# Prompt attention of a two-layer decoder step: transposes by half rows, the mask in the evictions, fixed engine orders

## The chip, the cores and the metric

The kernel runs on one core of a Trainium2 chip. The metric is the time of one execution on the device in microseconds (us); smaller is better. The kernel before the change took 3136.19 us (median of three runs, 3132.84 to 3143.44).

## The reference

One inference step of a small decoder for two groups of requests: one prompt of 1024 tokens behind 16 meta tokens, and eight samples of eight tokens each. Layer one is an mLSTM mixer, layer two a "forgetting attention" that reads one shared K and V; each is followed by a SwiGLU feed-forward part. The change touches the attention of the prompt alone:

```
# q, k, v: (1, 1040, 16 heads, 64); c = cumsum(log forget gate) over the positions
def one_block(qi, ci, pi):              # a block of 128 queries
    s = einsum('bqhd,bkhd->bhqk', qi, k)
    s = s + ci[..., None] - c[:, :, None, :]
    s = where(pos_k <= pi[:, None], s, -inf)
    return einsum('bhqk,bkhd->bqhd', softmax(s), v)
out = (o * sigmoid(og)) @ w_out
```

All data are float32. Only the 1024 prompt queries are computed in this stage; the queries of the 16 meta tokens come from the stage before.

## The kernel before

The program goes through the stages of both layers one after another; `attend_prompt` is the stage between the sample attention (`attend_sample`, with the sigmoid gates of the output as filler on TensorE) and the last output projection with its feed-forward part (`mlp`). q, k, the values, the negated decay sums `cD` and the gates `og2D` lie in DRAM scratch when it starts.

The 16 heads go in eight pairs `hp`: partitions 0 to 63 hold one head's 64 features, 64 to 127 the other's (`z` = 0, 1). The 1024 queries go in four groups `g` of two blocks `u` of 128, in the order `QG = (0, 3, 1, 2)`. Block `qb = 2g + u + 1` sees its first 16 + 128 qb keys; their last 128 are the diagonal.

Scores (`scores`, L1731 on). A block's keys are cut in pieces by `KSPLIT`, for example (400, 384) for `qb` 6. A piece is three matmuls per head (high times high, high times low, low times high part of q and k, L1751) into one PSUM bank per head, `sp0` and `sp1`, one place each. The piece with the diagonal gets two more matmuls per head (L1757), which add a mask of minus 1e30 through an identity. VectorE then evicts each head's piece with one instruction (L1759): it adds the decay row `ncb`, writes the score row `s` and carries the running maximum in `mx`. GpSimd makes the bias `nb` (L1768, L1769), ScalarE takes the exponential in place with the row sum in `sm` (L1771).

Products (`units`, L1775 on). A unit takes two columns of 128 keys (the last unit of a group: one, and the rest). Its first half, `turn`, transposes the 128x128 tiles of `s` on TensorE into PSUM (L1793, L1799), two units deep, and ScalarE copies them to `th` (L1796, L1807). In the last unit of a group the last 16 keys of each row are transposed from 32 partitions (L1803) and copied by VectorE (L1808). Its second half, `prod`, multiplies with the values into the bank `po` (L1816, L1820, and over 16 partitions L1824); at the end of a group VectorE makes the reciprocal `r` of the row sums (L1828), TensorE spreads it (L1831), VectorE multiplies by gate and `r` (`y`, L1834, L1835), and GpSimd splits the result in two parts for the next projection (L1843, L1844).

Order. TensorE's order is written out by hand (`manual_schedule` for TensorE): `ahead` keeps the score pieces nine pieces and more ahead of the products that use them, and per unit come score pieces, `turn`, score pieces, and the `prod` of the unit before. Below, S is a score piece, T a `turn`, P a `prod`. The order on VectorE, ScalarE and GpSimd is left to the framework's scheduler. `load` (L1709 on) brings a head pair's nine operands by SyncE's queue, into tiles that alternate between two places. At the start the last gate (`last_gate`, L1687 on) fills TensorE between the first nine score pieces.

Of the kernel before, what the change touches and what calls it, by code (L numbers as in the profile page):

```python
# [1667 lines left out]
def attend_prompt(self, ys):  # L1668
# [3 lines left out]
    with self.pool("ap", bufs=1) as sp, self.pool("ap2", bufs=2) as s2, self.pool("app", bufs=2, space=PSUM) as pp:  # L1672


        mask = sp.tile([P, 2, P], F32R, name="mneg")
        idr = sp.tile([P, 2, P], F32R, name="idr")
        tmp = sp.tile([P, 2, P], F32, name="mtmp")
        for dst, fill, op, sign in ((mask, NEG, ALU.is_ge, -1), (idr, 1.0, ALU.not_equal, -1)):
            nc.gpsimd.memset(tmp, 0.0)
            for a in range(2):  # L1680
                for h in range(2):
                    x = tmp[a * 64 : a * 64 + 64, h, :]
                    nc.gpsimd.affine_select(out=x, in_=x, compare_op=op, fill=fill, base=h * 64, pattern=[[sign, P]],
                                            channel_multiplier=1)
            nc.vector.tensor_copy(dst, tmp)

        def last_gate():  # L1687

            for t, (t0, t1) in enumerate(TS):
                n = t1 - t0  # L1690
                ps = pp.tile([P, 512], F32, name=f"og7{t}", tag="op")
# [4 lines left out]
                s = s2.tile([P, SL], F32, name=f"og7s{t}", tag="og7", bufs=1)  # L1696
                nc.scalar.activation(s[:, :n], ps[:, :n], AF.Sigmoid)
                nc.gpsimd.dma_start(self.og2D[7, :, t0:t1], s[:, :n])

        def first_tile():  # L1700

            og0 = sp.tile([P, KT, T0], F32, name="og0")
            nc.sync.dma_start(og0, self.og2D[:, :, :T0].rearrange("m p t -> p m t"))
            nc.vector.tensor_tensor(out=ys, in0=ys, in1=og0, op=ALU.mult)
            self.split(ys, self.X[0][0][:, :, :T0], self.X[0][1][:, :, :T0])

        heads = {}

        def load(hp):  # L1709
            cs = slice(hp * P, hp * P + P)  # L1710
            vr = s2.tile([P, 9, P], F32, name=f"vr{hp}", tag="vr")
            og = s2.tile([P, SEQ], F32, name=f"og{hp}", tag="ogP")
            kq = []
            for nm, d in (("q", self.qD), ("k", self.kD)):
                for z in range(2):
                    t = s2.tile([P, NP], F32R, name=f"{nm}{z}_{hp}", tag=f"{nm}{z}")
                    nc.sync.dma_start(t.bitcast(F32), d[z][hp])
                    kq.append(t)
            ncb = []
            for z in range(2):  # L1720
                t = s2.tile([P, NP], F32, name=f"ncb{z}_{hp}", tag=f"ncb{z}")
                nc.sync.dma_start(t, self.cD[2 * hp + z].partition_broadcast(P))
                ncb.append(t)
            nc.sync.dma_start(vr[:, :8, :], self.vD[: 8 * P, cs].rearrange("(j p) d -> p j d", p=P))
            nc.sync.dma_start(vr[:NM, 8, :], self.vD[8 * P :, cs])
            nc.sync.dma_start(og, self.og2D[hp, :, T0:])
            heads[hp] = (kq, ncb, vr, og)
# [3 lines left out]
        def scores(hp, g):  # L1731

            (qh, ql, kh, kl), ncb, _, _ = heads[hp]
            sm = s2.tile([P, 2, 2], F32, name=f"sm{hp}_{g}", tag="sm", bufs=4)
            ss = {}
            rows[hp, g] = (ss, sm)
            for u in range(2):
                qb = 2 * g + u + 1
                nk = NM + P * qb
                qs = slice(NM + P * (qb - 1), NM + P * qb)  # L1740
                for z in range(2):
                    ss[z, u] = s2.tile([P, nk], F32, name=f"s{hp}_{qb}_{z}", tag=f"s{qb}")
                mx = s2.tile([P, 2, 4], F32, name=f"mx{hp}_{qb}", tag="mx", bufs=4)
                at = 0
                for c, n in enumerate(KSPLIT[qb]):
                    ps = [pp.tile([P, 512], F32, name=f"sp{hp}_{qb}_{c}_{z}", tag=f"sp{z}", bufs=1) for z in range(2)]
                    diag = at + n == nk
                    for x, (a, b) in enumerate(((qh, kh), (qh, kl), (ql, kh))):
                        for z in range(2):
                            r = slice(z * 64, z * 64 + 64)  # L1750
                            nc.tensor.matmul(ps[z][:, :n], a[r, qs], b[r, at : at + n], start=(x == 0),  # L1751
                                             stop=(x == 2 and not diag))
                    if diag:
                        for x in range(2):
                            for z in range(2):
                                r = slice(z * 64, z * 64 + 64)
                                nc.tensor.matmul(ps[z][:, n - P : n], idr[r, x], mask[r, x], start=False, stop=(x == 1))  # L1757
                    for z in range(2):
                        nc.vector.tensor_tensor_reduce(  # L1759
                            out=ss[z, u][:, at : at + n], in0=ps[z][:, :n], in1=ncb[z][:, at : at + n], scale=1.0,  # L1760
                            scalar=NEG if c == 0 else mx[:, z, c - 1 : c], op0=ALU.add, op1=ALU.max,
                            accum_out=mx[:, z, c : c + 1])
                    at += n
                    if diag:

                        nb = s2.tile([P, 2], F32, name=f"nb{hp}_{qb}", tag="nb", bufs=4)
                        cq = self.cqP[:, qb - 1, 2 * hp : 2 * hp + 2]
                        nc.gpsimd.tensor_tensor(out=nb, in0=cq, in1=mx[:, :, c], op=ALU.subtract)  # L1768
# [6 lines left out]
        def units(hp, g):  # L1775

            _, _, vr, og = heads[hp]
            ss, sm = rows[hp, g]
            po = pp.tile([P, 512], F32, name=f"op{hp}_{g}", tag="op")
            nf = 2 * g + 1  # L1780
            out = []
            for j0 in range(0, nf, 2):
# [3 lines left out]
                def turn(j0=j0, tail=tail, hold=hold):  # L1786
                    pt = pp.tile([P, 2, 2, 256], F32, name=f"tp{hp}_{g}_{j0}", tag="tp")
                    th = s2.tile([P, 2, 2, 256], F32, name=f"th{hp}_{g}_{j0}", tag="th", bufs=3)
                    hold["th"] = th
                    for x in range(1 if tail else 2):  # L1790
                        for z in range(2):
                            for u in range(2):
                                nc.tensor.transpose(pt[:, x, z, u * P : u * P + P],  # L1793
                                                    ss[z, u][:, (j0 + x) * P : (j0 + x + 1) * P], self.ident)
                    if not tail:
                        nc.scalar.copy(th, pt)  # L1796
                        return
                    for z in range(2):
                        nc.tensor.transpose(pt[:, 1, 0, z * P : z * P + P], ss[z, 1][:, nf * P : (nf + 1) * P],  # L1799
                                            self.ident)  # L1800
                    for z in range(2):
                        for u in range(2):
                            nc.tensor.transpose(pt[:NM, 1, 1, (2 * z + u) * 32 : (2 * z + u) * 32 + 32],  # L1803
                                                ss[z, u][96:, (nf + u) * P : (nf + u) * P + NM],
                                                self.ident[96:, 96:])
# [125 lines left out]
```

## Time and profile before

| what | us |
| --- | --- |
| median of three runs | 3136.19 |
| the profiled execution, device time | 3134.74 |
| its span, first to last instruction | 3133.0 |
| prompt attention, first score matmul to last y product | 1892.8 to 2205.7 |

The profile shows one execution. A row of a timeline has the start in us from the span's start, the time covered, engine, line, instruction, tiles, shapes and count, and in brackets the idle time before it with what ended it. Neighbouring instructions of one kind are merged into one row, so the time covered reaches from the first one's start to the last one's end, and matmuls overlap in it. PE is TensorE, PEld its weight loads, DVE VectorE, ACT ScalarE, POOL GpSimd, SPq SyncE's DMA issues. A row of groups has busy time and mean duration in ns, then the idle time before. A row of waits has the total, the number and the longest.

In the stage TensorE's row is full: of the 40 us from 1972 to 2012 it is busy for 40.00, VectorE for 19.78, ScalarE for 23.87, GpSimd for 8.26, and the granted clock is 1.00.

### The profile page before, as it was taken

The numbers are of one execution on the slowest core, as the hardware profiler recorded it, in microseconds if no ns is written. First come the engines' busy times: TensorE is split into PE (matmuls) and PEld (weight loads), VectorE is DVE, ScalarE is ACT, GpSimd is POOL, SyncE is SP. The second block draws the span as 40 slices with busy tenths as digits, with TensorE's granted clock in tenths as the row PEclk, the third lists the DMA queues.
The fourth block names the chain that finished last, engine by engine and source line by source line (L and its number), as shares of the span: only waits on it lengthen the run. The fifth ranks groups of instructions, "written<-read, shape, count | busy, mean of one in ns | idle before, by whom it ended". The sixth has DMA issues, their size and how long they took to land.

```text
span 3133.0 us, 50924 instructions
## 1 busy us (share of the span) xinstructions
PE 3034.0 (97%) x21182; PEld 2883.1 (92%) x21182; DVE 1265.6 (40%) x2678; ACT 950.2 (30%) x1873; POOL 412.2 (13%) x806
## 2 busy tenths in 40 slices
PE   7999989999999999999999998999999999999998
PEld 7998879999999999999999886777999999999998
DVE  5132545633333333272455433554453333333323
ACT  5122453311111111142445445666331111111112
POOL 2011322100000000044453011222210000000002
PEclk9999999999999999999999998999999999999999
DMA  6142544111111111134444854332311111111111
GB/s 212 33 117 82 140 120 123 47 48 41 45 43 41 48 41 48 41 112 141 152 156 126 297 207 167 110 124 75 113 48 41 47 41 43 45 41 48 41 41 58
DMA packets 243314, 277.85 MB, mean 89 GB/s; under 512 B 26510, under 2 KB 193866, under 8 KB 243082
## 3 DMA queue, kind: packets, MB, share of 16 engines
q1 hardware_dynamic: 215426, 195.88, 19.9%
q0 software_dynamic: 23984, 76.40, 7.5%
q8 instruction: 166, 2.72, 0.4%
q10 hardware_dynamic: 3672, 2.31, 0.3%
q14 instruction: 66, 0.54, 0.1%
HBM read 211.35 MB, written 63.18 MB: 88 GB/s over the span
## 4 chain that ended last, share of the span: by engine, by line
PE 79%; DVE 4%; ACT 2%; DMA 2%; issue 1%; POOL 0%; SPq 0%; ACTq 0%; DVEq 0%; POOLq 0%
PE fps L63 11%; PE fps L62 11%; PE fps L64 11%; PE dps L62 5%; PE dps L63 5%; PE dps L64 5%; PE tmps L62 3%; PE tmps L63 3%; PE tmps L64 3%; PE sp L1751 3%; PE tp L1793 2%; PE op L1816 2%; PE pops L64 2%; PE pops L63 2%; PE pops L62 2%
## 5 line engine op out<-in xcount | busy, mean ns | idle before, releaser
L133 DVE TENSOR_TENSOR slot<-slot,slot 128x1024 fp32r<-128x1024 f32 x140 | 171.9, 1229 | 483.7 <-ACT slot L132 483.6
L132 ACT CAST slot<-slot 128x1024 fp32r<-128x1024 f32 x140 | 147.1, 1051 | 707.9 <-PE dps L63 393.7
L62 PE MATMUL dps<-ah,slot 128*128 128x384 f32 (+1 forms) x1056 | 353.1, 334 | 6.1 <-DVE vA L1075 3.1
L63 PE MATMUL dps<-al,slot 128*128 128x384 f32 (+1 forms) x1056 | 349.1, 331 | 0.0
L64 PE MATMUL dps<-ah,slot 128*128 128x384 f32 (+1 forms) x1056 | 348.7, 330 | 0.0
L205 POOL TENSOR_TENSOR ns<-ns,nq 128x384 f32<-128x384 f32 (+1 forms) x72 | 80.9, 1123 | 1717.6 <-ACT nq L203 1717.5
L62 PE MATMUL fps<-x1h,slot 128*128 128x384 f32 x704 | 236.9, 337 | 0.0
L62 PE MATMUL fps<-x2h,slot 128*128 128x384 f32 x704 | 236.5, 336 | 0.0
L63 PE MATMUL fps<-x2l,slot 128*128 128x384 f32 x704 | 236.5, 336 | 0.0
L64 PE MATMUL fps<-x2h,slot 128*128 128x384 f32 x704 | 236.5, 336 | 0.0
L64 PE MATMUL fps<-x1h,slot 128*128 128x384 f32 x704 | 236.5, 336 | 0.0
L63 PE MATMUL fps<-x1l,slot 128*128 128x384 f32 x704 | 236.4, 336 | 0.0
L64 PE MATMUL fps<-x0h,slot 128*128 128x336 f32 x704 | 223.0, 317 | 0.0
L62 PE MATMUL fps<-x0h,slot 128*128 128x336 f32 x704 | 222.5, 316 | 0.0
L63 PE MATMUL fps<-x0l,slot 128*128 128x336 f32 x704 | 222.4, 316 | 0.0
L62 PEld LDWEIGHTS dps<-ah,slot 128*128 128x128 f32 x1056 | 198.3, 188 | 13.9 <-DVE vA L1075 6.6
L63 PEld LDWEIGHTS dps<-al,slot 128*128 128x128 f32 x1056 | 198.5, 188 | 0.2
L64 PEld LDWEIGHTS dps<-ah,slot 128*128 128x128 f32 x1056 | 198.3, 188 | 0.0
L1053 DVE TENSOR_TENSOR fs<-fps,fs 128x336 f32<-128x336 f32 x132 | 71.4, 541 | 282.7 <-PE fps L64 282.7
L1075 DVE TENSOR_TENSOR Ht<-Ht,dps 128x384 f32<-128x384 f32 (+1 forms) x240 | 125.7, 536 | 106.0 <-PE dps L64 106.0
L1075 DVE TENSOR_TENSOR vA<-vA,dps 128x384 f32<-128x384 f32 (+1 forms) x240 | 125.4, 535 | 91.2 <-PE dps L64 91.2
L132 ACT CAST ah<-fs 128x336 fp32r<-128x336 f32 x132 | 65.7, 498 | 282.0 <-DVE fs L1053 282.0
(560 smaller groups left out, 7335.2 us busy)
## 6 DMA issues: line engine op xcount, KB each, us to landing
slot<-in_w_gate_up SPq DMA_DIRECT2D x88, 512.0 KB
slot<-in_w_down SPq DMA_DIRECT2D x44, 512.0 KB
kp<-in_cache_k SPq DMA_DIRECT2D x32, 512.0 KB
vp<-in_cache_v SPq DMA_DIRECT2D x32, 512.0 KB
wraw<-in_w_in_a SPq DMA_DIRECT2D x24, 512.0 KB
ncb<-cD SPq DMA_DIRECT2D x16, 520.0 KB
slot<-in_w_qo_b SPq DMA_DIRECT2D x16, 512.0 KB
slot<-in_w_kvf SPq DMA_DIRECT2D x14, 512.0 KB
```

Of the source, the lines that this page charges most:

```text
L62: mm(ps, sh, mh, start=first, stop=False)
L63: mm(ps, sh, ml, start=False, stop=False)
L64: mm(ps, sl, mh, start=False, stop=last)
L132: self.nc.scalar.copy(hi, src)
L133: self.nc.vector.tensor_tensor(out=lo, in0=src, in1=hi.bitcast(F32), op=ALU.subtract)
L205: (nc.vector if x == KT - 1 else nc.gpsimd).tensor_tensor(out=s, in0=s, in1=sq, op=ALU.add)
L1053: nc.vector.tensor_tensor(out=s[:, :n], in0=ps[:, :n], in1=s[:, :n], op=ALU.mult)
L1075: nc.vector.tensor_tensor(out=H[t][:, m], in0=H[t][:, m], in1=o, op=ALU.add)
L1751: nc.tensor.matmul(ps[z][:, :n], a[r, qs], b[r, at : at + n], start=(x == 0), stop=(x == 2 and not diag))
L1793: nc.tensor.transpose(pt[:, x, z, u * P : u * P + P], ss[z, u][:, (j0 + x) * P : (j0 + x + 1) * P], self.ident)
L1816: mm(po[ds[z], :256], vr[:, j0 + x, ds[z]], th[:, x, z], start=(j0 + x == 0), stop=False)
```

## The change

- Every 128x128 transpose becomes two of 64 rows by 128 columns, the upper and the lower half of the queries, which write to two PSUM banks. One ScalarE copy takes both banks to `th`.
- The four matmuls of the mask go. A tile `nd` holds the last 128 decay values of a block plus the mask; GpSimd makes it three blocks ahead (`masked`). The piece with the diagonal is evicted in two instructions per head, the part before the diagonal and the diagonal.
- The last 16 keys: the small transposes become ordinary matmuls over 64 partitions with a part of the identity; ScalarE copies them into `tails`, zero below row 16; values and weights are then multiplied over all 128 partitions.
- Three score places shared by both heads instead of one each; one product bank instead of two.
- VectorE, ScalarE and GpSimd are ordered by hand as well: they take their instructions in the order of the text.
- `load` is split into `load_k` (q, k, decay) and `load_v` (values, gates in quarters), issued at other points; the first tiles are allocated ahead in a set order; the last gate uses the places of `tp` and `th`; the gating of the sample rows (`first_tile`) is split in two calls; `y` is written over the gate.

```diff
+        tails = [sp.tile([P, P], F32, name=f"tail{x}") for x in range(2)]
...
+        def load_k(hp, e):
+            kq = first.pop(0) if first else place_k(hp)
+            ncb = firstc.pop(0) if firstc else place_c(hp)
+            for t, d in zip(kq, (self.qD[0], self.kD[0], self.kD[1], self.qD[1])):
+                e.dma_start(t.bitcast(F32), d[hp])
+            e.dma_start(ncb, self.cD[2 * hp : 2 * hp + 2].partition_broadcast(P))
+            heads[hp] = (kq, ncb)
...
+        def load_v(hp, e):
             cs = slice(hp * P, hp * P + P)
...
+            e.dma_start(vr[:, :8, :], self.vD[: 8 * P, cs].rearrange("(j p) d -> p j d", p=P))
+            nc.gpsimd.memset(vr[:, 8, :], 0.0)
+            e.dma_start(vr[:NM, 8, :], self.vD[8 * P :, cs])
...
+        def masked(x):
+            if x < len(blocks):
+                hp, qb = blocks[x]
+                d = diag[x] = s2.tile([P, 2, P], F32, name=f"nd{hp}_{qb}", tag="nd", bufs=4) if x else nd
+                nk = NM + P * qb
+                nc.gpsimd.tensor_tensor(out=d, in0=heads[hp][1][:, :, nk - P : nk],
+                                        in1=mask.unsqueeze(1).broadcast_to([P, 2, P]), op=ALU.add)
...
+                x = blocks.index((hp, qb))
+                masked(x + 3)
...
+                    ps = [pp.tile([P, 512], F32, name=f"sp{hp}_{qb}_{c}_{z}", tag="sp", bufs=3) for z in range(2)]
...
-                    if diag:
-                        for x in range(2):
-                            for z in range(2):
-                                r = slice(z * 64, z * 64 + 64)
-                                nc.tensor.matmul(ps[z][:, n - P : n], idr[r, x], mask[r, x], start=False, stop=(x == 1))
+                    parts = [(0, n)] if at + n < nk else [(0, n - P), (n - P, n)]
                     for z in range(2):
...
+                        for y, (o, e) in enumerate(parts):
+                            nc.vector.tensor_tensor_reduce(
+                                out=ss[z, u][:, at + o : at + e], in0=ps[z][:, o:e],
+                                in1=diag[x][:, z] if y else ncb[:, z, at + o : at + e], scale=1.0,
+                                scalar=mx[:, z, c + y - 1 : c + y] if c + y else NEG, op0=ALU.add, op1=ALU.max,
+                                accum_out=mx[:, z, c + y : c + y + 1])
...
+            po = pp.tile([P, 512], F32, name=f"op{hp}_{g}", tag="op", bufs=1)
...
+                    for y, (z, u, j) in enumerate(ts):
+                        for h in range(2):
+                            r = slice(h * 64, h * 64 + 64)
+                            nc.tensor.transpose(pt[:, h, y], ss[z, u][r, j * P : j * P + P], self.ident[r, r])
+                    if tail:
                         for z in range(2):
                             for u in range(2):
+                                nc.tensor.matmul(pt[:NM, 1, 6 + z, u * 32 : u * 32 + 32],
+                                                 ss[z, u][64:, (nf + u) * P : (nf + u) * P + NM],
+                                                 self.ident[64:, 96:], start=True, stop=True)
+                    n = len(ts)
+                    nc.scalar.copy(th.rearrange("p x z (u h q) -> p h (x z u) q", h=2, q=64)[:, :, :n], pt[:, :, :n])
+                    if tail:
+                        nc.scalar.copy(tw[:NM], pt[:NM, 1, 6:].rearrange("p a q -> p (a q)"))
...
+                            mm(po[ds[z], u * P + 96 : u * P + P], vr[:, nf + u, ds[z]], tw[:, c : c + 32],
                                start=False, stop=(u == 1))
...
-        with tc.manual_schedule(engines={mybir.EngineType.PE}):
-            load(0)
+        with tc.manual_schedule(engines={E.PE, E.DVE, E.Activation, E.Pool}):
```

More of the change, by code (lines that the diff above doesn't have):

```diff
@@ L1672, in attend_prompt @@
     with self.pool("ap", bufs=1) as sp, self.pool("ap2", bufs=2) as s2, self.pool("app", bufs=2, space=PSUM) as pp:
[L1675 to L1685, printed above, removed]
+        mask = sp.tile([P, P], F32, name="mneg")
+        nc.gpsimd.memset(mask, 0.0)
+        nc.gpsimd.affine_select(out=mask, in_=mask, compare_op=ALU.is_ge, fill=NEG, base=0, pattern=[[-1, P]],
+                                channel_multiplier=1)
+        tails = [sp.tile([P, P], F32, name=f"tail{x}") for x in range(2)]
+        for x in tails:
+            nc.gpsimd.memset(x, 0.0)
+        nd = s2.tile([P, 2, P], F32, name="nd0", tag="nd", bufs=4)
+        w7f = [w.bitcast(F32).rearrange("p k n -> p (k n)") for w in self.w7]
         def last_gate():
@@ L1739, in scores @@
                 nk = NM + P * qb
+                x = blocks.index((hp, qb))
+                masked(x + 3)
                 qs = slice(NM + P * (qb - 1), NM + P * qb)
                 for z in range(2):
[L1742 to L1748, printed above, removed]
+                    ss[z, u] = firsts.pop((qb, z)) if (qb, z) in firsts else row(hp, qb, z)
@@ L1795, in turn @@
[L1795 to L1805, printed above, removed]
@@ L1875, in attend_prompt @@
             for hp, g in groups:
-                if g == QG[0] and hp < 7:
-                    load(hp + 1)
                 us = None
```

111 lines of the change are left out of this document (65 added, 46 removed).

## The prediction

> **What bounds the kernel now.** I read the page first.
>
> ```profile
> PE 3034.0 (97%) x21182; PEld 2883.1 (92%) x21182; DVE 1265.6 (40%) x2678; ACT 950.2 (30%) x1873; POOL 412.2 (13%) x806
> ```
>
> TensorE is busy nearly throughout, but this is an average over stages. The prompt attention is the stretch in which the lines of the change run. Its length per pair of heads ("a head pair", eight of them) comes from the timeline of SyncE: the same load is issued once per head pair.
>
> ```profile
> 1972.81 0.32 SPq L1717 DMA_DIRECT2D q<-qDh  x1
> 2008.40 0.32 SPq L1717 DMA_DIRECT2D q<-qDh  x1
> ```
>
> That is 35.6 us per head pair, 285 us for eight. Inside one, the timeline of 2000 to 2012 us shows the blocks S (a score piece), T (the transposes of one unit) and P (the products of one unit):
>
> ```profile
> 2000.08 0.81 PE L1751 MATMUL sp<-k,q 64*128 64x400 f32 x6
> ...
> 2000.82 1.09 PE L1793 MATMUL tp<-ident,s 128*128 128x128 f32 x8
> ...
> 2001.84 0.85 PE L1751 MATMUL sp<-k,q 64*128 64x256 f32 x5
> ...
> 2002.91 0.65 PE L1816 MATMUL op<-th,vr 128*64 128x256 f32 x4
> ...
> 2003.39 0.39 PE L1820 MATMUL op<-th,vr 128*64 128x128 f32 x4
> ...
> 2003.71 0.42 PE L1824 MATMUL op<-th,vr 16*64 16x32 f32 x8
> ...
> 2004.06 0.66 PE L1831 MATMUL op<-ident,r 128*64 128x128 f32 x8
> ...
> 2004.65 1.09 PE L1793 MATMUL tp<-ident,s 128*128 128x128 f32 x8
> ...
> 2007.43 1.12 PE L1751 MATMUL sp<-k,q 64*128 64x384 f32 x6
> ...
> 2008.22 0.50 PE L1757 MATMUL sp<-mneg,idr 64*128 64x128 f32 x4
> ...
> 2008.65 1.09 PE L1793 MATMUL tp<-ident,s 128*128 128x128 f32 x8
> ...
> 2009.67 1.08 PE L1816 MATMUL op<-th,vr 128*64 128x256 f32 x8
> ...
> 2010.69 0.56 PE L1751 MATMUL sp<-k,q 64*128 64x144 f32 x6
> ...
> 2011.08 0.38 PE L1757 MATMUL sp<-mneg,idr 64*128 64x128 f32 x4
> ...
> 2011.39 0.66 PE L1793 MATMUL tp<-ident,s 128*128 128x128 f32 x4
> ```
>
> A block's price is the distance from its start to the next block's. No block waits long for another engine: TensorE's own sequence sets the pace. Eight transposes take 1.02 us from start to next block; their own row, less the last one's tail of 0.27 us, gives some 0.11 us between starts, 0.87 for eight. The other 0.15 us is the entry into a block of another array shape (128*128 after 64*128). Whether the 64-row matmuls of S run two abreast, a full-array stream of about the same width shows:
>
> ```profile
> 1909.06 0.33 PE L64 MATMUL og<-x1h,wlo 128*128 128x384 f32 x1
> 1909.23 0.33 PE L62 MATMUL og<-x1h,whi 128*128 128x384 f32 x1
> ```
>
> One costs 0.17 us, so six in a row 1.0 us; the six of 400 columns at 2000.08 took 0.74. They do run in pairs, three times 0.175, and 0.21 us is the entry into S.
>
> **The change on TensorE, per head pair.** Counting the emission order of the loops (unchanged): 72 tiles of 128x128 are transposed, 8 blocks of scores end in a mask, 4 groups have a last unit, and on average T follows S 5.6 times and S follows T 7.4 times.
>
> - Half rows: 72 tiles at 0.11 become 72 pairs of 64 columns, 0.055 if the halves run abreast as S's do. Saved 3.9; bounds 0 (no overlap) and 3.9.
> - T takes S's array shape, so entries between them go: 5.6 x 0.15 + 7.4 x 0.21 = 2.4. From S or T into P and out they stay.
> - Masks off TensorE: four matmuls took 0.31 us at 2011.08 with T's entry, about 0.2 without; eight blocks, 1.6.
> - Last keys in full rows: L1820 and L1824 take 0.32 and 0.35 us, each with a shape change behind it; in one shape 0.21 and 0.22. That and the shape change inside T save 1.4 for four groups; the small transposes as full fp32 products (two passes) give 0.5 back. Net 0.9.
>
> Together 8.8 us. Three score places can also take the present waits for a free place:
>
> ```profile
> PEld sp L1751 <- DVE mx L1759: 8.5, 38, 0.6
> ```
>
> This is the view of waits of 1932 to 2200 us, total, times and longest: 1.1 us per head pair. With everything else hidden, a head pair would take 35.6 - 8.8 - 1.1 = 25.7 us.
>
> **What is late next.** VectorE, ScalarE and GpSimd now take their work in the order of the text. These rows show what that moves:
>
> ```profile
> 2008.66 0.62 DVE L1759 CUSTOM_DVE_ANT_0 s<-sp,ncb,mx 128x384 f32<-128x384 f32 x1 [0.95 <-PE sp L1751]
> ...
> 2009.20 0.61 DVE L1759 CUSTOM_DVE_ANT_0 s<-sp,ncb,mx 128x384 f32<-128x384 f32 x1
> ...
> 2009.74 0.09 DVE L1759 DVE_READ_ACCUMULATOR2_ANT mx<- 128x1 f32 x1
> 2009.84 1.01 ACT L1796 COPY th<-tp 128x1024 f32<-128x1024 f32 x1 [2.72 <-PE tp L1793]
> ...
> 2010.24 0.20 POOL L1769 TENSOR_TENSOR nb<-nb,cqP 128x2 f32<-128x2 f32 x1
> ...
> 2010.74 0.95 ACT L1771 ACTIVATE s<-s,nb 128x784 f32<-128x784 f32 x1
> ```
>
> The T block of 2008.65 is copied out at 2009.84, ahead of the two exponentials of the S block that TensorE did before it. In the text those exponentials stand first. In fixed order the copy starts when they end: S ends at 2008.66; evictions, maximum and bias take until 2010.44, 1.8 us; two exponentials 1.9; the copy 1.0; 4.7 in all. The diagonal now has an eviction of its own for each head. What that costs comes from
>
> ```profile
> 2011.59 0.31 DVE L1759 CUSTOM_DVE_ANT_0 s<-sp,ncb 128x144 f32<-128x144 f32 x1 [1.77 <-issue]
> ...
> 2011.82 0.30 DVE L1759 CUSTOM_DVE_ANT_0 s<-sp,ncb 128x144 f32<-128x144 f32 x1
> ```
>
> 0.23 us apart for 144 columns against 0.54 for 384: 1.3 ns a column by this pair at most, and at least 0.04 us for an instruction by itself. The new one also starts from the maximum that the one before it has just written, which no row shows between neighbours; I take 0.1 each (bounds 0.04 and 0.23), 0.2 per block. So 4.9 us from the end of S to the copied T, while TensorE reaches the product of this T after: T 0.44, P 1.02 with its entry 0.15, S of 144 columns 0.39, T of the last unit 0.33 + 0.24, S of 272 columns 0.35, entry 0.1: 3.0. **TensorE waits 1.9 us.** Two more places per head pair have the exponentials of a long row just ahead of the copy:
>
> ```profile
> L1771 ACT ACTIVATE s<-s,nb 128x1040 f32<-128x1040 f32 x16 | 18.5, 1158 | 0.1
> ...
> L1771 ACT ACTIVATE s<-s,nb 128x912 f32<-128x912 f32 x16 | 16.8, 1050 | 2.3 <-POOL nb L1769 2.3
> ...
> L1807 ACT COPY th<-tp 128x768 f32<-128x768 f32 x32 | 25.3, 791 | 22.2 <-PE tp L1803 22.2
> ```
>
> After the row of 912: chain 2.2 (behind the y products on VectorE) + 2.1 + 0.8 + 0.1 = 5.2, work 3.3: 1.9. After that of 1040: 2.15 + 2.3 + 1.0 + 0.1 = 5.5, work 3.1: 2.4. Sum of the three 6.2. At the other five blocks the product is 4 to 5 us behind, and I count nothing (up to 0.5 each if the chain is longer).
>
> ```profile
> 2000.61 0.17 DVE L1828 RECIPROCAL r<-sm 128x4 f32<-128x4 f32 x1
> ```
>
> This reciprocal ran 3.4 us before its matmuls at 2004.06. In text order it stands behind the evictions of the S before its P: 0.2 + 1.2 + 0.27 = 1.7 us after that S ends, while TensorE is there after 1.0. That is 0.7, 0.6 and 0.6 at three groups (the fourth already waits above), 1.8. Where only a T lies between two S, the second head's matmul waits for the third place, 0.5 once net of the waits above. Given back: 6.2 + 1.8 + 0.5 = 8.5 us. A head pair takes 34.2, **1.4 us less, 11 us for eight**.
>
> Other moves that I cost at nothing. One product bank instead of two: between the last product of a group and the first of the next stand at least a T and an S with their entries, 1.2 us by the prices above, and the two y products have to fit in there; bounds 0 and 0.5 at four groups, 0 taken because y stands ahead of those evictions on VectorE. ScalarE takes over VectorE's copy of 16 rows; that lies outside the three chains (bounds 0 and 0.3 a group). The loads of a head pair become 11 DMAs instead of 9 on SyncE's queue, keys ahead of values and each asked for half a head pair or more before its use; the short value load now waits for a memset on GpSimd, and behind it only the four gate loads and the next keys wait, which have that half head pair of cover. Seven of the eight `affine_select` calls and two casts of the old masks go, ahead of the stage, where GpSimd is idle. The sample's gating (og0) is split in two calls; its VectorE and ScalarE work is the same.
>
> **The start of the stage.** The first scores wait for their loads:
>
> ```profile
> 1887.61 0.32 SPq L1717 DMA_DIRECT2D q<-qDl  x1
> ...
> 1892.76 0.49 PE L1751 MATMUL sp<-k,q 64*128 64x144 f32 x2 [4.56 <-DMA k<-kDh]
> ...
> 1895.17 0.70 PE L1751 MATMUL sp<-k,q 64*128 64x144 f32 x4 [1.93 <-DMA k<-kDl]
> ```
>
> 6.5 us of waiting; the second load could be issued only once its place was free. The change gives the first tiles places of their own choice in another order of allocation, so this can vanish, or return at another tile. I take 4 us saved (bounds -3 and 7).
>
> **The sum.** 3134.7 us in the profiled execution - 11 - 4 = **3120 us**. That execution lies 1.5 us below the median of 3136.2, inside the runs' own spread of 10.6 us, and I leave that difference out.
>
> A rule on the half rows stands in the Trainium skill, "TensorE: Matmul & The Clock Gate", section "LDWEIGHTS (loading the stationary operand)": the load's time goes by the columns alone, so half the rows load as slowly as all. By its P / 1.2, 128 columns cost an estimated 107 ns, a pair of halves would be no faster than one whole tile, and the term of 3.9 us would be 0. The rows are between:
>
> ```profile
> L1751 PEld LDWEIGHTS sp<-k,q 64*128 64x128 f32 x672 | 59.6, 191 | 38.1 <-issue 18.4 <-DVE mx L1759 13.1 <-DMA k<-kDl 2.1
> L1793 PEld LDWEIGHTS tp<-ident,s 128*128 128x128 f32 x512 | 56.0, 143 | 16.5 <-issue 14.0
> ```
>
> S's 64-row loads are no shorter (191 ns) than the whole-tile loads of T (143 ns); T's are the shorter ones by 48 ns, which leaves room for halves every 0.055 us.
>
> **Rivals.** (1) *TensorE keeps its gain.* If the copies are not late (the order on ScalarE lets them pass, or the chain is 2 us shorter), 70 us of shapes, halves and masks and 4 to 8 of waits stay: 3062. For it, the longest wait of TensorE for a copy at present:
>
> ```profile
> PEld op L1816 <- ACT th L1807: 2.1, 8, 0.3
> ```
>
> Against it: the order of the text and the three chains above. (2) *Slower: GpSimd in the chain.* Each block gets a masked tile on GpSimd, 256 columns a row, as long as
>
> ```profile
> L1844 POOL TENSOR_TENSOR x0l<-y,x0h 128x256 fp32r<-128x256 f32 x8 | 5.8, 731 | 0.6
> ```
>
> In fixed order these 0.73 us and y's casts can stand before the bias of a block. If so, every one of about six late copies moves by 0.7 and more: 4.4 us per head pair, 3.0 beyond the gain of 1.4, and 3144 to 3155. It decides from 1.4 us per head pair, 0.25 us at each place. Against: the masked tile is asked for three blocks ahead. (3) *The halves gain nothing*, by the load rule: TensorE's sequence is 3.9 longer, but T also fills the windows of the late copies, so only 0.7 of it shows; 3126.
>
> **How the numbers follow.** Forecast (3105 to 3132) 0.52, rival 1 0.17, rival 2 0.16, rival 3 0.15. A measurement here can tell 0.3%, 9.4 us, from no change. Two thirds of the forecast, rival 1 and a quarter of rival 3 are faster by more: 0.56; rival 2 is slower by more for most of its weight, with a little of the others: 0.17; the rest, 0.27, within. The range takes in the forecast, rival 3, most of rival 2 and the nearer part of rival 1: 3070 to 3150; the likeliest case alone has 3105 to 3132.
>
> **What would show it.** Right: transposes in pairs with about 0.055 us per tile, S and T without the entry; a product's first matmul waiting 1.5 to 2.5 us for ScalarE's copy three times per head pair; the matmuls of r waiting for VectorE; ScalarE idle ahead of its exponentials with a finished T behind them; loads issued 34.2 us apart. Wrong: 26 to 29 us apart with TensorE still without waits (rival 1), or GpSimd's masked tiles ending just before the bias (rival 2).

## The result and the profile after

The changed kernel takes 3159.99 us (median of four runs, 3157.15 to 3167.53); the kernel before took 3135.07 beside it (3132.84 to 3143.44). The ratio is 1.0078, with an interval of 1.0053 to 1.0104: slower by 25 us. Forecast were 3120, and 3070 to 3150 as the range. The profiled execution took 3157.15.

First the page, the row of busy times:

```profile
PE 3001.0 (95%) x21630; PEld 2861.4 (91%) x21630; DVE 1289.1 (41%) x2900; ACT 951.1 (30%) x1905; POOL 453.3 (14%) x872
```

TensorE works 33 us less than before and the span is 22 us longer: what it saved came back as pauses, and more. The load of a head pair's q, in SyncE's timeline (start first), shows where:

```profile
1933.29 0.32 SPq L1722 DMA_DIRECT2D qh<-qDh  x1
...
2123.68 0.32 SPq L1722 DMA_DIRECT2D qh<-qDh  x1
```

Five head pairs in 190.4 us, 38.1 each, against 35.7 before by the same loads and 34.2 in the forecast. The view of waits of TensorE from 1880 to 2240 us (total, times, longest) names the pauses:

```profile
PE op L1852 <- ACT th L1842: 35.9, 23, 3.0
PE op L1867 <- DVE r L1864: 10.9, 19, 0.7
PE sp L1787 <- DVE mxf L1791: 8.1, 1, 8.1
PE pops L62 <- ACT wo L132: 8.0, 1, 8.0
```

The first two are the products that wait for ScalarE's copy, and the matmuls that wait for the reciprocal: both forecast. The third is the start of the stage, the fourth its end, where the first product of the next stage waits for its weights; that one I had not seen. One late copy in the timeline of all engines:

```profile
2028.17 0.66 PE L1834 MATMUL tp<-ident,s 64*128 64x64 f32 x16
...
2030.58 0.20 POOL L1805 TENSOR_TENSOR nb<-nb,cqP 128x2 f32<-128x2 f32 x1
...
2030.81 1.16 ACT L1807 ACTIVATE s<-s,nb 128x1040 f32<-128x1040 f32 x1 [3.59 <-POOL nb L1805]
...
2031.97 1.15 ACT L1807 ACTIVATE s<-s,nb 128x1040 f32<-128x1040 f32 x1
...
2033.12 0.99 ACT L1842 COPY th<-tp 128x1024 f32<-128x1024 f32 x1
...
2034.16 0.44 PE L1852 MATMUL op<-th,vr 128*64 128x256 f32 x2 [1.63 <-ACT th L1842]
```

ScalarE sat idle for 3.59 us, since the bias was next in its order; then two exponentials, then the copy of the T of 2028.17, which TensorE had finished before all of them; the product waited 1.63 us. And the transposes themselves, in TensorE's timeline:

```profile
2039.60 0.66 PE L1834 MATMUL tp<-ident,s 64*128 64x64 f32 x16
2040.06 0.86 PE L1787 MATMUL sp<-kh,qh 64*128 64x256 f32 x2
```

Sixteen halves, that is eight tiles, in 0.46 us to the next block, where eight whole tiles took 1.02. So the gain on TensorE exists, and the question is where it went.

### The profile page after: what moved, and what is told of

Its sections match the earlier page's. It is cut to its first block, busy times and chain, and to the rows that moved or that the text cites. A ratio compares the mean times of both kernels' runs of the same rounds, so it can differ in the third digit from the quotient of the medians.

```text
span 3155.4 us, 52341 instructions
## 1 busy us (share of the span) xinstructions
PE 3001.0 (95%) x21630; PEld 2861.4 (91%) x21630; DVE 1289.1 (41%) x2900; ACT 951.1 (30%) x1905; POOL 453.3 (14%) x872
## 4 chain that ended last, share of the span: by engine, by line
PE 74%; DVE 6%; ACT 4%; issue 3%; DMA 2%; POOL 1%; DVEq 0%; SPq 0%; POOLq 0%; ACTq 0%
PE fps L63 11%; PE fps L62 11%; PE fps L64 11%; PE dps L62 5%; PE dps L63 5%; PE dps L64 5%; PE tmps L62 3%; PE tmps L63 3%; PE tmps L64 3%; PE pops L64 2%; PE pops L62 2%; PE pops L63 2%; DVE s L1791 2%; PE op L1852 1%; PE sp L1787 1%
## 5 line engine op out<-in xcount | busy, mean ns | idle before, releaser
L63 PE MATMUL dps<-al,slot 128*128 128x384 f32 (+1 forms) x1056 | 349.8, 331 | 0.0
L63 PE MATMUL fps<-x2l,slot 128*128 128x384 f32 x704 | 236.5, 336 | 0.0
L63 PE MATMUL fps<-x1l,slot 128*128 128x384 f32 x704 | 236.4, 336 | 0.0
L63 PE MATMUL fps<-x0l,slot 128*128 128x336 f32 x704 | 222.4, 316 | 0.0
L63 PEld LDWEIGHTS dps<-al,slot 128*128 128x128 f32 x1056 | 199.2, 189 | 0.2
```

Of the source, the lines that this page charges most:

```text
L63: mm(ps, sh, ml, start=False, stop=False)
```

## The experiments

Theory A: TensorE's own work became shorter; the fixed orders of ScalarE and VectorE give it back (copies behind exponentials, reciprocal behind evictions), and two tiles got places that come free late. Theory B, against it: the longer chain of split evictions, masked tile and bias is late whatever the order. Ratios are to the kernel before beside the same runs; "per head pair" is the mean distance of five loads as above.

| kernel | median us | ratio, 95% interval | per head pair us |
| --- | --- | --- | --- |
| after | 3159.99 | 1.0078 [1.0053, 1.0104] | 38.1 |
| e1_free_orders | 3094.27 | 0.9856 [0.9839, 0.9872] | 29.7 |
| e2_scalare_free | 3123.47 | 0.9949 [0.9933, 0.9966] | 33.2 |
| e3_heads_alternate | 3144.11 | 1.0019 [1.0006, 1.0033] | 36.7 |
| e4_before_fixed | 3182.54 | 1.0138 [1.0116, 1.0159] | 43.0 |
| f1_places | 3149.74 | 1.0037 [1.0021, 1.0053] | 38.6 |
| f2_no_mask | 3138.33 | 1.0016 [1.0003, 1.0029] | 35.8 |
| f3_no_gpsimd_tiles | 3151.96 | 1.0060 [1.0043, 1.0077] | 38.2 |
| g1_free_alt_places | 3082.32 | 0.9848 [0.9827, 0.9868] | 29.7 |
| h1_r_early | 3144.59 | 1.0022 [1.0004, 1.0040] | 36.5 |
| h2_free_whole | 3106.49 | 0.9910 [0.9884, 0.9936] | 32.6 |
| h3_free_pe_mask | 3087.51 | 0.9847 [0.9826, 0.9868] | 30.8 |
| h4_fixed_reordered | 3087.98 | 0.9861 [0.9836, 0.9886] | 29.7 |

**All three orders given back (e1).**

```diff
-        with tc.manual_schedule(engines={E.PE, E.DVE, E.Activation, E.Pool}):
+        with tc.manual_schedule(engines={E.PE}):
```

> The kernel after, with only TensorE ordered by hand in this stage; VectorE, ScalarE and GpSimd go back to the framework's order. Theory A (the fixed order puts copies behind exponentials and the reciprocal behind evictions; TensorE's own gain is there): the waits of the products for the copy (43.4 us in the stage) and of r's matmuls (13.1) go almost entirely, the granted clock returns from 0.92 towards 1.00, loads come 27 to 30 us apart, about 3085 us (3065 to 3110). Theory B (what is late is the chain of the split evictions, the masked tile and the bias, whatever the order): the waits stay above two thirds, 3140 to 3160.

3094, 66 us less than after and 1.4% faster than before. Its loads and its waits of TensorE (1880 to 2240 us):

```profile
1928.93 0.32 SPq L1722 DMA_DIRECT2D qh<-qDh  x1
...
2077.30 0.32 SPq L1722 DMA_DIRECT2D qh<-qDh  x1
```

```profile
PE sp L1787 <- DVE mxf L1791: 8.0, 1, 8.0
PE pops L62 <- ACT wo L132: 7.7, 1, 7.7
PE sp L1787 <- DVE mx L1791: 6.3, 15, 1.3
PE op L1852 <- ACT th L1842: 0.8, 1, 0.8
```

The 35.9 us for copies have become 0.8, the 10.9 for the reciprocal are gone; the start and the end stay. Theory A holds in its main point; B falls.

**ScalarE alone given back (e2).**

```diff
-        with tc.manual_schedule(engines={E.PE, E.DVE, E.Activation, E.Pool}):
+        with tc.manual_schedule(engines={E.PE, E.DVE, E.Pool}):
```

> The kernel after, with ScalarE alone given back to the framework's order. Theory A: the copies pass the exponentials, 43.4 us of waits go and part of the lost clock returns; r's 13 us stay: about 3105 us (3090 to 3125). Theory B: the exponentials still wait for the bias and the copies with them: 3145 to 3160.

3123, at the upper end of A's range. In the same view:

```profile
PE op L1867 <- DVE r L1864: 18.5, 28, 3.1
...
PE op L1852 <- ACT th L1842: 1.3, 2, 1.2
```

The copies are no longer late, but the reciprocal is later than in after (18.5 us against 10.9): with one pause gone TensorE is sooner at the next one. The 33.2 us per head pair hold one of 37.0 in which the granted clock fell to 0.8; the other four are 32.1 to 32.4. ScalarE's order is worth 36 us, those of VectorE and GpSimd 29 more.

**The reciprocal alone, earlier in the text (h1).**

```diff
# in turn, last unit, after the copy to tails
+                        hold["r"] = s2.tile([P, 2, 2], F32, name=f"r{hp}_{g}", tag="r")
+                        nc.vector.reciprocal(hold["r"], sm)
# in prod
-                    r = s2.tile([P, 2, 2], F32, name=f"r{hp}_{g}", tag="r")
-                    nc.vector.reciprocal(r, sm)
+                    r = hold["r"]
```

> The kernel after, with the reciprocal of a group's row sums issued in the last unit's transposes instead of after its products, in fixed order ahead of the evictions of the score piece between. Theory (the matmuls of r wait 13 us in the stage for a reciprocal that stands behind evictions, a term that the prediction had at 1.8 us per head pair): these waits go, 3147 to 3152. Rival (the late copies right behind take the time back): 3156 or more.

3145, 15 us less and a little under the theory's range. The waits of the matmuls of r are gone from the view, those for the copies are what they were (36.0 us against 35.9). One instruction a group, issued behind evictions that it has nothing to do with, cost 0.5% of the program.

**The split evictions head by head in turn (e3).**

```diff
-                    for z in range(2):
-                        for y, (o, e) in enumerate(parts):
+                    for y, (o, e) in enumerate(parts):
+                        for z in range(2):
```

> The kernel after, with the two parts of a split eviction taken head by head in turn (part before the diagonal of head 0, of head 1, then the diagonals), so that no eviction starts from the maximum that its direct neighbour has just written. If the dependent neighbour is what makes the four evictions of a block 1.5 us instead of some 1.1: 0.2 to 0.4 us less per block, at six late copies per head pair 1.2 to 2.4 us, 10 to 19 us for eight: about 3145. If the cost is the instructions themselves: within 5 us of 3160.

3144, as expected for the dependent neighbour. One block of 256 columns in VectorE's timeline, in after, then in e3, then in f2, where the eviction is undivided:

```profile
2036.69 0.35 DVE L1791 CUSTOM_DVE_ANT_0 s<-sp,ncb,mx 128x128 f32<-128x128 f32 x1 [3.30 <-PE sp L1787]
...
2037.19 0.35 DVE L1791 CUSTOM_DVE_ANT_0 s<-sp,nd,mx 128x128 f32<-128x128 f32 x1
...
2037.47 0.34 DVE L1791 CUSTOM_DVE_ANT_0 s<-sp,ncb,mx 128x128 f32<-128x128 f32 x1
...
2037.86 0.35 DVE L1791 CUSTOM_DVE_ANT_0 s<-sp,nd,mx 128x128 f32<-128x128 f32 x1
...
2038.13 0.17 DVE L1864 RECIPROCAL r<-sm 128x4 f32<-128x4 f32 x1
```

```profile
2029.16 0.35 DVE L1791 CUSTOM_DVE_ANT_0 s<-sp,ncb,mx 128x128 f32<-128x128 f32 x1 [2.81 <-PE sp L1787]
...
2029.43 0.35 DVE L1791 CUSTOM_DVE_ANT_0 s<-sp,ncb,mx 128x128 f32<-128x128 f32 x1
...
2030.25 0.17 DVE L1864 RECIPROCAL r<-sm 128x4 f32<-128x4 f32 x1
```

```profile
2030.79 0.48 DVE L1790 CUSTOM_DVE_ANT_0 s<-sp,ncb,mx 128x256 f32<-128x256 f32 x1 [4.70 <-PE sp L1786]
...
2031.20 0.48 DVE L1790 CUSTOM_DVE_ANT_0 s<-sp,ncb,mx 128x256 f32<-128x256 f32 x1
...
2031.60 0.17 DVE L1863 RECIPROCAL r<-sm 128x4 f32<-128x4 f32 x1
```

From the first eviction to the reciprocal behind the last: 1.44, 1.09 and 0.81 us. An independent neighbour starts 0.27 us after the one before it, one that needs its maximum 0.50 or 0.39. The split costs 0.63 us in this block, 0.35 of it by the dependence, where I had taken 0.2: it is 0.31 for each head, outside my bounds of 0.04 and 0.23.

**No mask (f2), no tiles by GpSimd (f3).**

```diff
# f2: undivided, and masked() is not called for the blocks
-                    parts = [(0, n)] if at + n < nk else [(0, n - P), (n - P, n)]
+                    parts = [(0, n)]
# f3: split as in after, one tile for all blocks
-                                in1=diag[x][:, z] if y else ncb[:, z, at + o : at + e], scale=1.0,
+                                in1=diag[0][:, z] if y else ncb[:, z, at + o : at + e], scale=1.0,
```

> The kernel after with the fixed orders, without the causal mask inside the diagonal: the last piece is evicted undivided, no masked tile is made. It shows what split evictions and masked tiles cost together. Theory (the split was mis-sized: about 0.6 us per block in place of 0.2, and every late copy moves with it): 0.5 to 0.6 us at some six places per head pair, 25 to 30 us less, about 3132. Rival (the fixed order alone makes the loss, the length of the evictions little): 3150 or more.

> The kernel after with the split evictions, but the masked tile of the first block is used for all blocks and GpSimd makes no other (the diagonals get the decays of block 1). Theory (the masked tiles are made ahead of need, the evictions are what lengthens the chain): 3152 to 3160. Rival 2 of the prediction (GpSimd's tile stands in the chain, 3 us per head pair): 3130 to 3140.

f2 leaves the mask out of the diagonal; in f3 every diagonal gets the decays of the first block's tile. f2 took 3138, between the two expectations but nearer to the theory's: 22 us less. The theory had every late copy move by 0.5 to 0.6 us; TensorE's waits for them are 32.4 us in f2, against 35.9 in after and 26.1 in e3, and those for the reciprocal 4.2, against 10.9 and 8.2. So the copies hardly moved, and how the shorter evictions bring the 22 us is not settled. f3 took 3152, at the lower end of the theory's range, and its loads lie as far apart as those of after: 38.2 us per head pair against 38.1; the intervals of the two ratios overlap. The masked tiles are off the path; rival 2 of the prediction falls.

**The places (f1).**

```diff
-        first = [place_k(0), place_k(1)]
+        first = [place_k(0)]
         firstv = [s2.tile([P, 9, P], F32, name="vr0", tag="vr")]
         firsto = [s2.tile([P, 256], F32, name="og0_0", tag="ogP", bufs=8)]
+        first.append(place_k(1))
...
-        firsts = {(qb, z): row(0, qb, z) for qb in (7, 6, 5, 1) for z in range(2)}
+        firsts = {(qb, z): row(0, qb, z) for qb in (7, 8, 3, 4, 1, 2) for z in range(2)}
```

> The kernel after, with its tiles allocated in another order only: the decays of the first heads get a place that the stage before doesn't use, and under the first two tiles of the next stage's weights lie q and k of the last head pair, which are done before the end. Theory (the places cost 7 to 8 us at the end of the stage, where TensorE waited 7.99 us for those weights, and some 5 at its start, where the evictions waited 10.2 us for the decays): 3145 to 3150. Rival (another wait is right behind each): 3155 to 3160.

3150: 10 us less. TensorE's waits (1880 to 2240 us) that stand for the 8.1 and 8.0 of after:

```profile
PE sp L1788 <- DVE mxf L1792: 4.7, 1, 4.7
...
PE pops L64 <- DVE wo L133: 1.6, 1, 1.6
```

In after the tiles of the next stage's first weights lay over values and gates of the last head pair, which are in use to the last product, and SyncE issues their load at 2220.16. Over q and k of that pair, done earlier, the load waits for a score matmul and is issued at 2199.68, and the wait of 8.0 us goes (of what follows it, 1.6 remain). At the start only 3.4 of 8.1 go; the load of the decays is still late there. In after it waits 16.6 us for the write of a gate from a tile of the stage before (SyncE's waits, `og2D<-ogb`), in f1 13.4 us for a gate matmul of that stage (`bps`, L63), so it seems that the stage before uses the new place as well.

**Fixed orders on the kernel before (e4).**

```diff
-        with tc.manual_schedule(engines={mybir.EngineType.PE}):
+        E = mybir.EngineType
+        with tc.manual_schedule(engines={E.PE, E.DVE, E.Activation, E.Pool}):
```

> The kernel before, with VectorE, ScalarE and GpSimd put in the order of the text as the change does, and nothing else of it. Theory A: the copies are late here too, by less, since TensorE's own work between a T and its P is about 1 us longer and the evictions are not split: 1 to 3 us per head pair, 3145 to 3160. Rival (the fixed order costs nothing by itself, only together with TensorE's shorter work): 3130 to 3140.

3183, slower by 1.4% and far over both expectations, and not by late copies. The waits of VectorE, then of TensorE, in the same stretch:

```profile
DVE th L1808 <- ACT th L1807: 71.9, 23, 4.6
```

```profile
PE sp L1751 <- DVE mx L1759: 22.2, 17, 4.4
...
PE op L1816 <- ACT th L1796: 2.7, 7, 1.6
```

VectorE's copy of the last 16 keys stands behind ScalarE's copy into the same tile; in fixed order the evictions behind it stand still, and the next scores find no free place. The kernel before has 42.6 us of this wait of VectorE, but TensorE waits only 3.1 us for a score place there. So a fixed text order costs here too, for the most part by another wait than in after; the change had taken this copy from VectorE.

**Free orders, with e3's and f1's edits (g1).** The diffs of e1, e3 and f1 together.

> The kernel after with three edits: VectorE, ScalarE and GpSimd in the framework's order, the split evictions head by head in turn, and the places of f1_places. If the three add up: 3094 less 13 for the places and up to 8 for the evictions (which are mostly covered without the fixed order): 3074 to 3084.

3082, 1.5% faster than before: the best median of the study. The loads are as far apart as in e1 (29.7 us); the gain over e1 is the two ends of the stage.

**Whole transposes in g1 (h2), mask on TensorE in g1 (h3).**

```diff
# h2 (the tile tp and the copy to match)
-                        for h in range(2):
-                            r = slice(h * 64, h * 64 + 64)
-                            nc.tensor.transpose(pt[:, h, y], ss[z, u][r, j * P : j * P + P], self.ident[r, r])
+                        nc.tensor.transpose(pt[:, y], ss[z, u][:, j * P : j * P + P], self.ident)
# h3: parts = [(0, n)], no masked tiles, and behind the three products of the last piece
+                        for y in range(2):
+                            for z in range(2):
+                                r = slice(z * 64, z * 64 + 64)
+                                nc.tensor.matmul(ps[z][:, n - P : n], idr[r, y], neg[r, y], start=False, stop=(y == 1))
```

> g1_free_alt_places with every tile transposed whole (128x128) as before the change. The trace of after gives 0.06 us per tile by halves against 0.11 whole, and a shape change of 0.15 to 0.17 us into and out of each unit of transposes besides. If the halves run abreast: 72 x 0.05 + some 1.2 = 4.8 us more per head pair, 38 for eight, about 3120 (3110 to 3128). If halves gain nothing by themselves (rival 3 of the prediction): the shapes alone, 3088 to 3095. If other engines set the pace without the fixed order: 3082 to 3088.

> g1_free_alt_places with the mask added on TensorE by four matmuls per block as before the change: no masked tile on GpSimd, diagonal evicted undivided. If TensorE's sequence is what a head pair costs in free order: eight blocks x 0.2 to 0.3 us, 13 to 19 us more, 3095 to 3102. If the split evictions and GpSimd's tiles cost as much as the four matmuls: 3080 to 3088.

h2: 3106, 24 us more, 2.9 us per head pair, between the ranges of the first two expectations; 38 were expected if all of it showed. Its timeline of TensorE:

```profile
2005.44 1.09 PE L1833 MATMUL tp<-ident,s 128*128 128x128 f32 x8
2006.46 0.51 PE L1788 MATMUL sp<-kh,qh 64*128 64x512 f32 x2
...
2009.29 0.35 PE L1788 MATMUL sp<-kh,ql 64*128 64x400 f32 x2
2009.57 0.44 PE L1833 MATMUL tp<-ident,s 128*128 128x128 f32 x2
```

1.02 us for eight tiles, as before the change. What TensorE gains by halves goes in part into waits for a free score place: 0.9 us of such waits in the whole stage of h2, 6.2 us in that of g1. h3 took 3088, in the second expectation; by the loads it takes 1.1 us more per head pair, 9 us for eight, while the ratios (0.9847 and 0.9848) show no difference. The four matmuls cost TensorE some 0.17 us a block, but they are not the 9 us. Those are a wait that g1 has for 1.7 us only:

```profile
PE op L1863 <- ACT th L1853: 10.2, 8, 1.4
```

What the matmuls cost comes back in shorter score pieces (table in the next section). Taking the mask off TensorE was worth little, and the time alone does not tell it from nothing.

**Fixed orders with another text (h4).** The diffs of e3, f1 and h1, and:

```diff
-                        for z in range(2):
-                            nc.scalar.activation(ss[z, u], ss[z, u], AF.Exp, bias=nb[:, z : z + 1],
-                                                 accum_out=sm[:, u, z : z + 1])
+                        pend.append((hp, g, exps))      # exps: the same two activations
# in turn: those of its own group at its start, the others after its copies
+                    flush((hp, g))
...
+                    flush()
```

> The kernel after with its fixed orders on all engines, but another text: exponentials of a block stand behind the copies of the next unit of transposes, the reciprocal as in h1, evictions head by head, places as in f1. Theory (the loss is the place of the exponentials ahead of the copies in the text): the waits for copies go, 3085 to 3100. Rival (any order fixed on all engines holds evictions, bias or copies back somewhere): 3110 or more.

3088, 29.7 us per head pair, with 0.8 us of waits for copies in the whole stage; 4.0 us of waits of a T for the exponentials ahead of it are new. All four engines are fixed as in after, and 72 us are back, by four edits: alone, the places brought 10, the heads in turn 16 and the reciprocal 15; the exponentials behind the copies weren't tried alone. So it is the order that the text gives, not that an order is fixed.

## Why the prediction was wrong, step by step

**Where the sign went.** The mechanism was the forecast one; two sizes were off, and one wait was missing. The sum of the prediction was 25.7 (TensorE alone) + 8.5 (given back) = 34.2 us per head pair, and 4 us saved at the start. Measured: 29.7 where the late copies and the late reciprocal are gone (e1 and g1 in free order, h4 in another text), and 38.1 - 29.7 = 8.4 given back. The step that failed is "With everything else hidden, a head pair would take 25.7 us", 4.0 too little, 32 us for eight. The start came out 1.6 us longer (8.1 against 6.5 of waiting) instead of 4 shorter, and the end of the stage, which the sum does not have, cost 8.0. 3120 + 32 + 5.6 + 8 = 3166, beside 3157 of the profiled execution; where these 9 us too many lie is open.

**TensorE alone.** The table has the distance from a block's first row to the next block's, from TensorE's timelines, added up over three head pairs (from one group's matmuls of r to the same ones three head pairs on) and divided by three. An entry or a wait ahead of a block counts with the block before it.

| us per head pair | before | e1 | h2 | h3 |
| --- | --- | --- | --- | --- |
| T | 9.36 | 5.36 | 9.34 | 5.24 |
| mask matmuls | 2.44 | | | 1.78 |
| S | 10.00 | 10.96 | 9.98 | 10.52 |
| small transposes, products, r | 14.00 | 13.33 | 13.31 | 13.29 |
| sum | 35.80 | 29.65 | 32.63 | 30.83 |

T and masks together fell by 6.4; forecast were 3.9 + 1.6 and 0.8 of entries into T, 6.3. The last keys fell by 0.7; forecast were 0.9. The score pieces are what failed: forecast were 1.6 of entries and 1.1 of waits less, and they take 1.0 more. That is 3.6 of the 4.0; 0.2 more is the start of the sum, 35.6 where this stretch has 35.8.

- Halves: right (72 pairs at 0.055 are 4.0; the 3.9 was a slip). 16 halves take 0.46 us where eight whole tiles take 1.02. The load rule (rival 3), by which they would gain nothing, doesn't hold here: h2 is 24 us slower. After's weight loads at the T of 2039.60:

```profile
2039.42 0.70 PEld L1834 LDWEIGHTS tp<-ident,s 64*128 64x128 f32 x16
```

  By the P / 1.2 of the Trainium skill ("TensorE: Matmul & The Clock Gate", section "LDWEIGHTS (loading the stationary operand)") a load of 128 columns is an estimated 107 ns, eight in a row 0.86 us. Here eight loads of upper and eight of lower rows are done within 0.70 us, and the next block starts 0.46 us after the T.
- Shape entries: 2.4 forecast, some 0.8 there. Into T they cost 0.10: in h2 the third pair of S takes 0.28 us to the next T (2009.29 to 2009.57), in e1 0.18. Into S they cost almost nothing. In e1's timeline stand an S behind a product and an S behind a T of its own shape:

```profile
2130.05 0.45 PE L1787 MATMUL sp<-kh,qh 64*128 64x400 f32 x2
2130.34 0.35 PE L1787 MATMUL sp<-kl,qh 64*128 64x400 f32 x2
2130.53 0.35 PE L1787 MATMUL sp<-kh,ql 64*128 64x400 f32 x2
2130.71 0.66 PE L1834 MATMUL tp<-ident,s 64*128 64x64 f32 x16
...
2133.67 0.71 PE L1834 MATMUL tp<-ident,s 64*128 64x64 f32 x16
2134.19 0.43 PE L1787 MATMUL sp<-kh,qh 64*128 64x400 f32 x2
2134.45 0.35 PE L1787 MATMUL sp<-kl,qh 64*128 64x400 f32 x2
```

  The first pair takes 0.29 behind the product, 0.26 behind the T, the next 0.19. Most of the 0.21 us that I called an entry is the first pair's own start, and stays: 5.6 x 0.10 + 7.4 x 0.03 = 0.8. The other runs agree: an S of 400 columns between a T and a product takes 0.75 us with whole tiles (before, h2) and 0.73 with halves (e1).
- Waits for a score place: 1.1 forecast to go. They grew: TensorE, being faster, meets the evictions. An S behind small transposes in e1:

```profile
2124.87 0.39 PE L1787 MATMUL sp<-kh,qh 64*128 64x272 f32 x1
...
2125.61 0.36 PE L1787 MATMUL sp<-kh,qh 64*128 64x272 f32 x1 [0.35 <-DVE mx L1791]
```

  Its product starts at 2126.15, 1.28 us after it; in h2 the same piece, where no wait shows, takes 0.57 (2003.85 to 2004.42). Four pieces per head pair are held up like this in e1: they take 1.29, 0.85, 1.49 and 1.02 us, where pieces of their sizes that aren't held up take 0.57, 0.57, 0.79 (h3) and 0.56. That makes 2.2 us; by the same reckoning it was some 1.3 before. The view of waits, which has 1.0 in e1 and 1.1 before, shows only a part.
- Masks: 1.6 forecast. The cost was right, but it bought nothing: h3, which has the matmuls and undivided evictions, spends 1.8 us per head pair on them, and its S, without the 1.4 us that its product waits for a copy, take 9.1 against 10.95 in g1. That points to the split evictions, which hold the score places longer, so that TensorE waits there instead; it rests on h3 and g1 alone.

**Given back.** 8.5 forecast, 8.4 measured, but the agreement is in part luck. At the first of the three places, in after:

```profile
2008.61 0.66 PE L1834 MATMUL tp<-ident,s 64*128 64x64 f32 x16
...
2014.17 1.11 PE L1852 MATMUL op<-th,vr 128*64 128x256 f32 x8 [1.83 <-ACT th L1842]
```

From the end of S (2008.61) to the product 5.6 us pass, where 4.9 were forecast; TensorE's own work in between is 3.7, where 3.0 were forecast. Two errors of 0.7 leave the wait at 1.83, against 1.9. The late copies cost 35.9 / 8 = 4.5 us of TensorE's waits per head pair (forecast 6.2), the reciprocal 1.4 (1.8); counted at the weight loads, where TensorE's pause begins, these are 5.4 and 1.6 (43.4 and 13.1 us in the stage). The remaining 1.4 is about what the clock takes (last section).

**Costed at nothing.** GpSimd's tiles: right (f3). The one product bank: right, no more than 0.7 us of waits for y in e1, in the whole stage. The loads of a head pair: right, no wait of TensorE for one stands in after's view. Allocation at the start: inside the bounds that I gave (-3 to 7), on the bad side. The end of the stage: the tiles that the next stage loads first lie where this stage's last tiles were; I had asked this question for the start alone.

**The rivals.** Rival 1 (TensorE keeps its gain) is what e1 and h4 are, at 3088 to 3094 and not 3062 (its own terms, 70 us and 4 to 8, give 3057 to 3061), for the reason given. Rival 2 named the right sign and the wrong place. Rival 3 falls with h2.

## What to carry to other kernels

When engines are put in the order of the text, the text is the schedule: for each instruction ask what stands ahead of it that waits for something later, above all a copy or a reciprocal behind work of another block; h4 and after have the same engines fixed and lie 72 us apart. For each piece of work taken off an engine, ask which wait it only lengthens (the masks here). Take the price of a block from the blocks that stay as well (is the "entry" there without a change of shape?), and where a tile's place moves, ask at both ends of the stage who had the place before and who gets it next.

## What the runs showed of the hardware

Where TensorE paused every few us, its granted clock was lower, which the forecast did not have. From 1932 to 2132 us, in windows of 40 us, it is 0.89 to 0.96 in after and 0.86 to 0.96 in e4, against 0.97 to 1.00 in the kernel before. Two stretches of after, in the view of windows; the clock granted is the number behind GpSimd's busy time:

```profile
2104.00:2110.00 6.00, 4.14 (x56) 2.93 (x53) 3.81 (x21) 3.70 (x6) 3.27 (x8) 1.00 0.09 23
2110.00:2116.00 6.00, 6.00 (x60) 4.40 (x58) 1.52 (x10) 3.35 (x11) 0.39 (x2) 0.56 0.02 3
```

In the last one TensorE is at 0.56, and its rows stretch with it. The same block 20 us earlier and in this stretch:

```profile
2094.82 0.66 PE L1867 MATMUL op<-ident,r 128*64 128x128 f32 x8 [0.39 <-DVE r L1864]
...
2114.75 1.12 PE L1867 MATMUL op<-ident,r 128*64 128x128 f32 x8
```

The head pair with this stretch took 39.8 us, the four before it 37.4 to 37.9. A shorter dip stands behind the longest wait of a head pair: T, S of 512 columns and four products, 1.87 us in e1 (2022.84 to 2024.71), take 3.33, 3.26 and 3.13 us in after (from 2015.21, 2052.90 and 2090.71), 1.3 to 1.5 more; a part of that comes off the short wait for r behind it. The Trainium skill ("TensorE: Matmul & The Clock Gate", section "HAM oscillation — how this bites in real kernels") asks for no idle gaps above about 3.4 us. Here the longest wait of TensorE in the 12 us ahead of the stretch at 0.56 is 1.63 us, so shorter ones in a row seem to be enough. In e1, where TensorE is busy for 38.7 of 40 us, the same view has 1.00 from 1960 to 2080 us. That the pauses cause it was not tried by itself. An eviction that starts from the maximum of its direct neighbour starts 0.12 to 0.23 us later than an independent one, and taking the heads in turn brought 16 us.
